# All ten gate pairs of each FFN as seven block products, with some low parts made by an accumulating DMA

## The chip, the core and the metric

The kernel runs on one core of one Trainium2 chip. The metric is device time in microseconds (us) of one launch, median over runs; lower is better.

## The reference, cut to what matters

The program is a trunk of two decoder layers in fp32, on 512 tokens of width 1024. Each layer has four groups of attention heads and then a dense SwiGLU feed-forward network (FFN) of inner width 2816. The change is in the FFN alone:

```python
h = rmsnorm(x, g_pre_ffn[l])
f = jax.nn.silu(jnp.einsum('bsd,df->bsf', h, w_gate[l])) * jnp.einsum('bsd,df->bsf', h, w_up[l])
f = jnp.einsum('bsf,fd->bsd', f, w_down[l])
x = x + rmsnorm(f, g_post_ffn[l])
```

## The kernel before, in words

**Split products.** Every fp32 matrix product is made of three matmuls on operands of type fp32r: each operand is split into a high part (a cast) and a low part (the operand minus its high part), and `mm3` (L195 to L198) adds high by high, high by low and low by high in PSUM. ScalarE (ACT) makes a weight block's high part `whi`, VectorE (DVE) its low part `wlo` (L172 in `weights`, L896 in `split_w`). A raw weight block `wraw` is 256 KB, loaded by a DMA of SyncE's queue (SP); five raw tiles and six `whi` and six `wlo` tiles rotate (WRAW, WSPL).

**The FFN of a layer.** The 2816 inner columns are 22 blocks of 128 (index `j`). Blocks 0 and 1 of gate and up come first, each in two halves of 256 tokens ("the halves"); the last of these four uses a weight tile `w_half` that lies in the tile slot `slotE`. The other 20 blocks are taken in pairs, a gate pair and then an up pair, and then comes the product with `w_down` (`ps_d`).

**A direct pair** is two calls of `block`: 2 x 8 contraction steps x 3 matmuls, 48 matmuls of 512 columns (PSUM tile `ps_g`).

**A pair as seven products** (`two_blocks`): the pair is a 2 x 2 grid of blocks (two halves of the contraction by two weight blocks a11, a12, a21, a22), and seven products p1, p5, p2, p6, p7, p3, p4, in this order, take the place of eight. Each is 4 contraction steps x 3 matmuls of 256 columns, so a pair is 84 (PSUM tile `ps_7`, named `ps` in the profile). Three products take a plain weight block (p1 takes a11, p2 a12, p4 a22); four take a sum s1 to s4, which DVE forms in `combine` (L901). DVE and ACT add the results up (L913, L920, L923). Before the change all ten up pairs of a layer and the five gate pairs with j = 4, 8, 12, 16, 20 go this way; the gate pairs with j = 2, 6, 10, 14, 18 are direct.

**The token side** of products p5, p6, p7 and p4 needs sums T1, T2, T3 and T4 of blocks of h. They are formed once a layer, between the halves and the first pair by seven products, in two rounds c = 0 and c = 1: POOL (GpSimd) adds h's high and low parts back (`back`, L866: b11, b12, b22, b21), DVE forms the differences (L876, L879, L881, L884), and `put` splits them (ACT L871, DVE L872). b11 and b12 have two tiles (NPART), so b12 of round 1 waits until round 0's T3 has been split; T3's tile lies in `slotE` and so waits for the last matmul of the halves.

**What sets the order.** A scheduler that works when the program is built fixes each engine's order; nothing is reordered on the chip. An engine that waits holds up everything behind it in its order.

Of the kernel before, what the change touches and what calls it, by code (L numbers as in the profile page):

```python
# [13 lines left out]
ALU = mybir.AluOpType  # L14
# [62 lines left out]
def f32(ap):  # L77
    return ap.bitcast(F32)
# [3 lines left out]
def decoder(ctx, tc, x, positions, w_in, b_forget, g_mla_q, w_mla_q_up, g_mla_kv, w_mla_kv_up,  # L82
            w_out, g_pre_mix, g_post_mix, w_gate, w_up, w_down, g_pre_ffn, g_post_ffn, consts, out):
    nc = tc.nc
# [5 lines left out]
    ps_mm = ctx.enter_context(tc.tile_pool(name="ps_mm", bufs=3, space=PSUM))  # L90
    ps_s = ctx.enter_context(tc.tile_pool(name="ps_s", bufs=2, space=PSUM))
    ps_t = ctx.enter_context(tc.tile_pool(name="ps_t", bufs=2, space=PSUM))
    ps_o = ctx.enter_context(tc.tile_pool(name="ps_o", bufs=1, space=PSUM))

    def bank(pool, name):
        return pool.tile([P, 512], F32, name=name, tag=pool.name)
# [10 lines left out]
    def H(name):  # L107
        return keep.tile([P, 512], F32, name=name, tag="part", bufs=NPART)
# [46 lines left out]

    chunk_no = [0]
    pool_share = [SHARE_MIX]

    def weights(src, shape, into=None):
        raw = wp.tile([P] + shape, F32, name="wraw", tag="wraw", bufs=WRAW)  # L160
        if into is None:
            hi = wp.tile([P] + shape, F32R, name="whi", tag="whi", bufs=WSPL)
            lo = wp.tile([P] + shape, F32R, name="wlo", tag="wlo", bufs=WSPL)
        else:
            hi, lo = into
        nc.sync.dma_start(raw, src)
        nc.scalar.copy(hi, raw)  # L167
        chunk_no[0] += 1
        if pool_share[0] and chunk_no[0] % pool_share[0] == 0:
            nc.gpsimd.tensor_tensor(lo, raw, f32(hi), op=ALU.subtract)  # L170
        else:
            nc.vector.tensor_tensor(lo, raw, f32(hi), op=ALU.subtract)  # L172
        return hi, lo
# [21 lines left out]
    def mm3(ps, a_hi, a_lo, b_hi, b_lo, start, stop):  # L195
        nc.tensor.matmul(ps, a_hi, b_hi, start=start, stop=False)  # L196
        nc.tensor.matmul(ps, a_hi, b_lo, start=False, stop=False)  # L197
        last_mm[0] = nc.tensor.matmul(ps, a_lo, b_hi, start=False, stop=stop)  # L198
# [620 lines left out]
    def ffn(l, xt, h, turns, f_slots, ahead, after):  # L819
# [5 lines left out]
        def w_of(src, j, into=(None, None)):  # L825
            cs = slice(j * P, (j + 1) * P)
            return [weights(src[l, 4 * i * P:4 * (i + 1) * P, cs].rearrange("(k p) c -> p k c", p=P), [4, P], into=into[i])
                    for i in range(2)]

        def block(ps, w, hs):  # L830
            for k in range(KD):
                hi, lo = w[k // 4]
                mm3(ps[:, hs], hi[:, k % 4, :], lo[:, k % 4, :], h[0][k // 4][:, k % 4, hs], h[1][k // 4][:, k % 4, hs],
                    k == 0, k == KD - 1)
# [52 lines left out]
        def raw_of(src, j, i):  # L887
            raw = wp.tile([P, 4, P], F32, name="wraw", tag="wraw", bufs=WRAW)
            nc.sync.dma_start(raw, src[l, 4 * i * P:4 * (i + 1) * P, j * P:(j + 1) * P].rearrange("(k p) c -> p k c", p=P))
            return raw  # L890

        def split_w(raw):
            hi = wp.tile([P, 4, P], F32R, name="whi", tag="whi", bufs=WSPL)
            lo = wp.tile([P, 4, P], F32R, name="wlo", tag="wlo", bufs=WSPL)
            nc.scalar.copy(hi, raw)  # L895
            nc.vector.tensor_tensor(lo, raw, f32(hi), op=ALU.subtract)  # L896
            return hi, lo

        def combine(a, b, op):
            s = T(F32, "wsum").rearrange("p (k c) -> p k c", c=P)  # L900
            nc.vector.tensor_tensor(s, a, b, op=op)  # L901
            return s

        def product(pool, w, n):
            ps = bank(pool, "ps_7")[:, 0:256]
            for k in range(4):
                mm3(ps, w[0][:, k, :], w[1][:, k, :], ops[n][0][k], ops[n][1][k], k == 0, k == 3)
            return ps

        def two_blocks(src, j, d1, d2):  # L910

            def add(to, a, b):
                nc.vector.tensor_tensor(to, a, b, op=ALU.add)  # L913

            c11, c12, c21, c22 = [d[:, s] for d in (d1, d2) for s in half]
            a11 = raw_of(src, j, 0)
            a21, a22 = raw_of(src, j + 1, 0), raw_of(src, j + 1, 1)
            a12 = raw_of(src, j, 1)
            p1 = product(ps_mm, split_w(a11), "11")
            nc.scalar.copy(c12, p1)  # L920
            s1 = combine(a21, a22, ALU.add)
            p5 = product(ps_s, split_w(s1), "T1")
            nc.scalar.copy(c22, p5)  # L923
            p2 = product(ps_o, split_w(a12), "21")
            add(c11, p2, c12)
            s2 = combine(s1, a11, ALU.subtract)
            p6 = product(ps_mm, split_w(s2), "T2")
            add(c12, p6, c12)
            s3 = combine(a11, a21, ALU.subtract)
            p7 = product(ps_t, split_w(s3), "T3")  # L930
            add(c21, p7, c12)
            s4 = combine(a12, s2, ALU.subtract)
            add(c12, c12, c22)
            add(c22, c22, c21)
            p3 = product(ps_s, split_w(s4), "22")
            add(c12, p3, c12)
            p4 = product(ps_t, split_w(a22), "T4")
            add(c21, p4, c21)

        for j in range(KF):  # L940
            if j < 2:
                (pg, _), (pu, _) = halves[2 * j:2 * j + 2]
            elif j - j % 2 in (4, 8, 12, 16, 20):
                if j % 2 == 0:
                    two_blocks(w_gate, j, fq[j], fq[j + 1])
                pg = fq[j]
            else:
                wg, pg = w_of(w_gate, j), bank(ps_mm, "ps_g")
                block(pg, wg, slice(0, 512))
            f = fq[j]  # L950
            nc.scalar.activation(f, pg, AF.Silu)
            if j < 2:
                nc.vector.tensor_tensor(f, f, pu, op=ALU.mult)
            elif j % 2 == 1:
                u = H("u1"), H("u2")
                two_blocks(w_up, j - 1, *u)
                for i in range(2):
                    f = fq[j - 1 + i]
                    nc.vector.tensor_tensor(f, f, u[i], op=ALU.mult)
# [56 lines left out]
    for c in range(2):  # L1016
        pg = bank(ps_s, "gain")
# [21 lines left out]
    for l in range(depth):  # L1039
# [9 lines left out]
        def after(t, turn):  # L1049
# [7 lines left out]
            if l + 1 < depth:  # L1057
# [9 lines left out]
                nxt_turns[t] = turn_next  # L1067

        ffn(l, xt, h, turns, set_a, ahead, after)
        if nxt:  # L1070
            h = nxt[1]
# [22 lines left out]
```

## Time and profile before

| | us |
|---|---|
| median of 3 runs (1240.09 to 1242.71) | 1241.17 |
| the profiled execution, its own time | 1241.33 |
| its span, first to last instruction | 1239.5 |

The profile's page gives the busy time of each engine over that span. PE is TensorE's matmuls, PEld its weight loads, DVE is VectorE, ACT ScalarE, POOL GpSimd, SP SyncE. A matmul's shown duration overlaps the next one's, so the pitch of matmuls is read from their starts.

### The profile page before, as it was taken

What the parts mean: (1) busy time and instruction counts of PE and PEld (TensorE: products, weight loads), DVE (VectorE), ACT (ScalarE), POOL (GpSimd) and SP (SyncE); (2) the same over time, 40 slices, a digit from 0 to 9 for tenths busy, and PEclk for the clock granted to TensorE, in tenths of its full rate; (3) what the DMA queues carried; (4) which work ended last, traced back from release to release, by engine and by line L of the source; (5) the groups of instructions that cost most, each with busy time, mean ns of one, the idle gap of its engine ahead of it and who ended that gap; (6) DMA issues with size and microseconds to landing.
All of it is one profiled execution on the core that took longest, in us unless ns stands there. A gap on an engine that the chain in (4) does not pass through costs nothing.

```text
span 1239.5 us, 20756 instructions
## 1 busy us (share of the span) xinstructions
PE 1211.5 (98%) x7372; PEld 1069.6 (86%) x7372; DVE 890.6 (72%) x1802; ACT 666.9 (54%) x1453; POOL 245.0 (20%) x337
## 2 busy tenths in 40 slices
PE   8999999989999999999999999999899999999997
PEld 7878877779999999888798888778799999998886
DVE  6877877778987888533667678766788987893334
ACT  6676766754554445332547677666454444453232
POOL 3343444343000000000242434333420000000001
PEclk9999999999999999999999999999999999999999
DMA  7221242521433333533622123233224333343331
GB/s 233 76 61 43 70 117 71 162 68 35 135 96 103 111 103 94 152 95 102 186 84 52 43 69 98 73 116 106 69 69 129 111 94 103 104 117 113 102 91 71
DMA packets 158060, 121.68 MB, mean 98 GB/s; under 512 B 9090, under 2 KB 133122, under 8 KB 157956
## 3 DMA queue, kind: packets, MB, share of 16 engines
q1 hardware_dynamic: 151908, 111.55, 30.9%
q10 hardware_dynamic: 6048, 8.80, 2.7%
q8 instruction: 58, 0.95, 0.3%
q14 instruction: 46, 0.38, 0.1%
HBM read 111.93 MB, written 4.19 MB: 94 GB/s over the span
## 4 chain that ended last, share of the span: by engine, by line
PE 83%; DVE 6%; ACT 4%; issue 2%; DMA 2%; POOL 2%; ACTq 0%; DVEq 0%; POOLq 0%
PE ps L197 8%; PE ps L196 8%; PE ps L198 8%; PE ps_d L197 6%; PE ps_d L198 6%; PE ps_d L196 6%; PE ps_g L197 4%; PE ps_g L196 4%; PE ps_g L198 3%; PE ps_qk L196 3%; PE ps_s L462 3%; PE ps_qk L197 3%; PE ps_qk L198 3%; PE pT L486 2%; PE ps_o L494 1%
## 5 line engine op out<-in xcount | busy, mean ns | idle before, releaser
L172 DVE TENSOR_TENSOR wlo<-wraw,whi 128x512 fp32r<-128x512 f32 x206 | 156.2, 767 | 133.2 <-ACT whi L167 130.7
L167 ACT CAST whi<-wraw 128x512 fp32r<-128x512 f32 (+1 forms) x224 | 135.7, 620 | 170.7 <-PE ps_d L198 117.9
L895 ACT CAST whi<-wsum 128x512 fp32r<-128x512 f32 x120 | 74.3, 620 | 133.4 <-DVE wsum L901 46.5
L197 PE MATMUL ps<-sum,whi 128*128 128x256 f32 x480 | 135.8, 283 | 0.0
L196 PE MATMUL ps<-sum,whi 128*128 128x256 f32 x480 | 135.5, 282 | 0.0
L198 PE MATMUL ps<-sum,wlo 128*128 128x256 f32 x480 | 135.3, 282 | 0.0
L196 PE MATMUL ps_d<-whi,fh 128*128 128x512 f32 x288 | 112.2, 390 | 0.0
L197 PE MATMUL ps_d<-wlo,fh 128*128 128x512 f32 x288 | 112.1, 389 | 0.0
L198 PE MATMUL ps_d<-whi,fl 128*128 128x512 f32 x288 | 112.0, 389 | 0.0
L198 PE MATMUL ps<-h,wlo 128*128 128x256 f32 x360 | 101.9, 283 | 0.0
L197 PE MATMUL ps<-h,whi 128*128 128x256 f32 x360 | 101.9, 283 | 0.0
L196 PE MATMUL ps<-h,whi 128*128 128x256 f32 x360 | 101.8, 283 | 0.0
L477 POOL TENSOR_SCALAR pr<-pr,den 128x128 f32<-128x128 f32 (+3 forms) x128 | 75.7, 608 | 115.1 <-DVE den L474 85.2
L198 PEld LDWEIGHTS ps<-sum,wlo 128*128 128x128 f32 x480 | 91.9, 192 | 0.0
L196 PEld LDWEIGHTS ps<-sum,whi 128*128 128x128 f32 x480 | 91.8, 191 | 0.0
L197 PEld LDWEIGHTS ps<-sum,whi 128*128 128x128 f32 x480 | 91.8, 191 | 0.0
L896 DVE TENSOR_TENSOR wlo<-wsum,whi 128x512 fp32r<-128x512 f32 x120 | 80.9, 683 | 9.5 <-ACT whi L895 8.4
L197 PE MATMUL ps_g<-h,whi 128*128 128x512 f32 (+1 forms) x224 | 81.3, 363 | 5.8 <-DVE h L225 5.8
L196 PE MATMUL ps_g<-h,whi 128*128 128x512 f32 (+1 forms) x224 | 81.1, 363 | 0.9 <-ACT h L225 0.8
L198 PE MATMUL ps_g<-h,wlo 128*128 128x512 f32 (+1 forms) x224 | 80.6, 360 | 0.0
L895 ACT CAST whi<-wraw 128x512 fp32r<-128x512 f32 x90 | 55.8, 620 | 42.6 <-PE ps L197 27.5
L196 PE MATMUL ps_qk<-h,whi 128*128 128x512 f32 x192 | 76.5, 398 | 0.0
(330 smaller groups left out, 3437.8 us busy)
## 6 DMA issues: line engine op xcount, KB each, us to landing
wraw<-in_w_gate_dram SPq DMA_DIRECT2D x88, 256.0 KB, 3.5
wraw<-in_w_up_dram SPq DMA_DIRECT2D x88, 256.0 KB, 3.1
wraw<-in_w_down_dram SPq DMA_DIRECT2D x88, 256.0 KB, 2.9
wraw<-in_w_in_dram SPq DMA_DIRECT2D x72, 256.0 KB, 3.1
wraw<-in_w_out_dram SPq DMA_DIRECT2D x32, 256.0 KB, 2.8
xt<-in_x_dram SPq DMA_DIRECT2D x16, 256.0 KB, 3.7
rope_b<-rope_a ACTq DMA_DIRECT2D x64, 64.0 KB, 2.0
wraw<-in_w_in_dram SPq DMA_DIRECT2D x16, 178.0 KB, 2.9
```

The lines of the kernel that those rows point to most:

```text
L167: nc.scalar.copy(hi, raw)
L172: nc.vector.tensor_tensor(lo, raw, f32(hi), op=ALU.subtract)
L196: nc.tensor.matmul(ps, a_hi, b_hi, start=start, stop=False)
L197: nc.tensor.matmul(ps, a_hi, b_lo, start=False, stop=False)
L198: last_mm[0] = nc.tensor.matmul(ps, a_lo, b_hi, start=False, stop=stop)
L462: nc.tensor.matmul(ps[:, 0:w], a[:, qt * P:(qt + 1) * P], b[:, 0:w], start=i == 0, stop=i == n - 1)
L477: nc.gpsimd.tensor_scalar(p, p, den[:, t - qa:t - qa + 1], 1.0, op0=ALU.mult, op1=ALU.mult)
L486: nc.tensor.transpose(pt[:, i * P:(i + 1) * P], pr[:, offs[qt] + kt * P:offs[qt] + (kt + 1) * P], ident)
L494: nc.tensor.matmul(o, v, mh, start=kt == 0, stop=False)
L895: nc.scalar.copy(hi, raw)
L896: nc.vector.tensor_tensor(lo, raw, f32(hi), op=ALU.subtract)
```

## The change

The five direct gate pairs of each layer become pairs by seven products too, the first of them (j = 2) right behind the halves. And the low part of a plain block in `split_w` is no longer DVE's subtraction: ACT writes the negated high part (raw times -1, rounded to fp32r on writing) into `wlo`, and a DMA issued by POOL adds the raw block onto it.

```diff
+    def low_by_dma(lo, raw):
+        nc.scalar.mul(lo, raw, -1.0)
+        nc.gpsimd.dma_start(lo, raw, accum_op=ALU.add)
...
-        def split_w(raw):
+        def split_w(raw, plain=False):
...
             nc.scalar.copy(hi, raw)
-            nc.vector.tensor_tensor(lo, raw, f32(hi), op=ALU.subtract)
+            if plain:
+                low_by_dma(lo, raw)
+            else:
+                nc.vector.tensor_tensor(lo, raw, f32(hi), op=ALU.subtract)
             return hi, lo
...
-            p1 = product(ps_mm, split_w(a11), "11")
+            p1 = product(ps_mm, split_w(a11, True), "11")
...
-            p2 = product(ps_o, split_w(a12), "21")
+            p2 = product(ps_o, split_w(a12, True), "21")
...
-            p4 = product(ps_t, split_w(a22), "T4")
+            p4 = product(ps_t, split_w(a22, True), "T4")
...
-            elif j - j % 2 in (4, 8, 12, 16, 20):
+            else:
                 if j % 2 == 0:
                     two_blocks(w_gate, j, fq[j], fq[j + 1])
                 pg = fq[j]
-            else:
-                wg, pg = w_of(w_gate, j), bank(ps_mm, "ps_g")
-                block(pg, wg, slice(0, 512))
```

The lines of the changed kernel stand four further down from `low_by_dma` on, so L871, L895, L866 are L875, L899, L870 there.

Where instructions move. First ACT, in layer 0 right behind the halves; sum1 to sum4 are the tiles of T1, T2, T3, T4, `whi` cast from `wsum` is a sum's high part, `whi` from `wraw` a plain block's. Before:

```order
L871 CAST sum3_3519<-b12_3528 128x512
L871 CAST sum1_3518<-t1_3551 128x512
L895 CAST whi_3678<-wsum_3676 128x512
L895 CAST whi_3696<-wraw_3656 128x512
L871 CAST sum3_3519<-b12_3549 128x512
L871 CAST sum2_3520<-b11_3547 128x512
L951 ACTIVATE f_3243<-ps_g_3584 128x512
L871 CAST sum4_3523<-b21_3563 128x512
```

and now:

```order
L875 CAST sum3_3519<-b12_3528 128x512
L927 COPY f_3243<-ps_7_3585 128x256
L875 CAST sum1_3518<-t1_3551 128x512
L899 CAST whi_3601<-wsum_3599 128x512
L899 CAST whi_3619<-wraw_3578 128x512
L875 CAST sum3_3519<-b12_3549 128x512
L875 CAST sum2_3520<-b11_3547 128x512
L875 CAST sum4_3523<-b21_3563 128x512
L160 ACTIVATE wlo_3620<-wraw_3578 128x512
L899 CAST whi_3640<-wsum_3638 128x512
L930 COPY f_3243<-ps_7_3605 128x256
L899 CAST whi_3660<-wsum_3658 128x512
```

The eviction of p1 (L927), the cast of a12 (wraw_3578) and, behind round 1's T casts, the negation of a12 (L160) now stand among the T casts; before, the silu of a direct block stood there.

POOL in the same place, before:

```order
L866 TENSOR_TENSOR b21_3542<-h_2924,h_2926 128x512
L866 TENSOR_TENSOR b11_3547<-h_2923,h_2925 128x512
L866 TENSOR_TENSOR b12_3549<-h_2923,h_2925 128x512
L866 TENSOR_TENSOR b22_3555<-h_2924,h_2926 128x512
L866 TENSOR_TENSOR b21_3563<-h_2924,h_2926 128x512
```

and now:

```order
L870 TENSOR_TENSOR b21_3542<-h_2924,h_2926 128x512
L161 DMA wlo_3581<-wraw_3572 128x512
L870 TENSOR_TENSOR b11_3547<-h_2923,h_2925 128x512
L870 TENSOR_TENSOR b12_3549<-h_2923,h_2925 128x512
L870 TENSOR_TENSOR b22_3555<-h_2924,h_2926 128x512
L870 TENSOR_TENSOR b21_3563<-h_2924,h_2926 128x512
L161 DMA wlo_3620<-wraw_3578 128x512
L161 DMA wlo_3701<-wraw_3576 128x512
```

The accumulating DMA of a11 stands between the two rounds of additions, that of a12 behind the second.

PE right behind p1 of that first pair, now (ps_7_3605 is p5, ps_7_3624 p2, ps_7_3644 p6, ps_7_3664 p7); where nothing but matmuls of the direct pair stood before:

```order
L200 MATMUL ps_7_3605<-sum1_3518,whi_3601 128x256 [waits Activation_49]
L201 MATMUL ps_7_3605<-sum1_3518,whi_3601 128x256 [waits DVE_49]
L200 MATMUL ps_7_3624<-h_2924,whi_3619 128x256 [waits DVE_49,Activation_49]
L201 MATMUL ps_7_3624<-h_2926,whi_3619 128x256
L202 MATMUL ps_7_3605<-sum1_3518,wlo_3602 128x256 [waits DVE_49]
```

and nine matmuls of p5 further on:

```order
L200 MATMUL ps_7_3644<-sum2_3520,whi_3640 128x256 [waits Activation_49]
L201 MATMUL ps_7_3644<-sum2_3521,whi_3640 128x256
L200 MATMUL ps_7_3664<-sum3_3519,whi_3660 128x256 [waits Activation_49]
L202 MATMUL ps_7_3624<-h_2924,wlo_3620 128x256 [waits DMASW1_49]
L200 MATMUL ps_7_3624<-h_2924,whi_3619 128x256
```

PE's third matmul of p5 waits for DVE's low part of s1, and the third of p2 for the accumulating DMA (semaphore DMASW).

## Rows read from the trace of the kernel before

**Rows 1.** The page's parts 1, 2 and 4: engines, granted clock, chain by engine.
```profile
PE 1211.5 (98%) x7372; PEld 1069.6 (86%) x7372; DVE 890.6 (72%) x1802; ACT 666.9 (54%) x1453; POOL 245.0 (20%) x337
...
PEclk9999999999999999999999999999999999999999
...
PE 83%; DVE 6%; ACT 4%; issue 2%; DMA 2%; POOL 2%; ACTq 0%; DVEq 0%; POOLq 0%
```

**Rows 2.** Windows, the stretch of three pairs by seven products, one direct pair before and after.
```profile
348.80:379.00 30.20, 30.20 (x254) 30.20 (x253) 26.64 (x52) 16.12 (x30) 0.00 (x0) 1.00 0.37 107
```

**Rows 3.** Timeline, PE: first matmul of a direct pair, of the sevens, and again.
```profile
296.73 0.40 PE L196 MATMUL ps_g<-h,whi 128*128 128x512 f32 x1
...
307.63 0.28 PE L196 MATMUL ps<-h,whi 128*128 128x256 f32 x1
...
337.79 0.39 PE L196 MATMUL ps_g<-h,whi 128*128 128x512 f32 x1
...
378.85 0.39 PE L196 MATMUL ps_g<-h,whi 128*128 128x512 f32 x1
```

**Rows 4.** Timeline, POOL, layer 0: start us, us, engine, line, operation, [idle before].
```profile
293.51 1.69 POOL L866 TENSOR_TENSOR b<-h 128x512 f32<-128x512 f32 x1 [3.64 <-DVE sum L872]
298.83 4.24 POOL L866 TENSOR_TENSOR b<-h 128x512 f32<-128x512 f32 x3 [3.63 <-DVE sum L872]
```

**Rows 5.** Timeline, DVE, the same stretch.
```profile
297.48 0.67 DVE L953 TENSOR_TENSOR f<-f,ps_u 128x512 f32<-128x512 f32 x1
298.08 0.68 DVE L872 TENSOR_TENSOR sum<-b,sum 128x512 fp32r<-128x512 f32 x1
300.15 1.76 DVE L876 TENSOR_TENSOR t<-b,b 128x512 f32<-128x512 f32 x1 [1.40 <-POOL b L866]
301.84 1.78 DVE L901 TENSOR_TENSOR wsum<-wraw 128x512 f32<-128x512 f32 x1
303.54 0.68 DVE L879 TENSOR_TENSOR b<-b,b 128x512 f32<-128x512 f32 x1
...
305.96 0.69 DVE L884 TENSOR_TENSOR b<-b,b 128x512 f32<-128x512 f32 x1
...
307.16 0.69 DVE L896 TENSOR_TENSOR wlo<-wsum,whi 128x512 fp32r<-128x512 f32 x1
```

**Rows 6.** Timeline, ACT, the same stretch.
```profile
296.98 0.62 ACT L871 CAST sum<-b 128x512 fp32r<-128x512 f32 x1 [0.23 <-PE ps_u L198]
301.95 0.62 ACT L871 CAST sum<-t 128x512 fp32r<-128x512 f32 x1 [4.34 <-DVE t L876]
303.65 0.62 ACT L895 CAST whi<-wsum 128x512 fp32r<-128x512 f32 x1 [1.08 <-DVE wsum L901]
...
304.70 1.38 ACT L871 CAST sum<-b 128x512 fp32r<-128x512 f32 x2
...
306.68 0.62 ACT L871 CAST sum<-b 128x512 fp32r<-128x512 f32 x1
```

**Rows 7.** Timeline, layer 1: POOL, then DVE.
```profile
909.93 4.24 POOL L866 TENSOR_TENSOR b<-h 128x512 f32<-128x512 f32 x3 [3.63 <-DVE sum L872]
...
911.25 1.77 DVE L876 TENSOR_TENSOR t<-b,b 128x512 f32<-128x512 f32 x1 [1.40 <-POOL b L866]
```

**Rows 8.** DMA view from 300 to 500 us, then the page's part 6.
```profile
q1 hardware_dynamic: 38356, 20.20, 35.1%
...
wraw<-in_w_up_dram SPq DMA_DIRECT2D x36, 256.0 KB, 3.0
wraw<-in_w_gate_dram SPq DMA_DIRECT2D x35, 256.0 KB, 3.4
...
rope_b<-rope_a ACTq DMA_DIRECT2D x64, 64.0 KB, 2.0
```

**Rows 9.** Groups by line and shape, ACT.
```profile
L895 ACT CAST whi<-wraw 128x512 fp32r<-128x512 f32 x90 | 55.8, 620 | 42.6 <-PE ps L197 27.5 <-ACT u L920 4.4 <-ACT f L951 4.0
...
L230 ACT ACTIVATE hn<-xt 128x512 f32<-128x512 f32 x32 | 20.2, 631 | 23.9 <-DVE xt L767 14.2 <-DVE xt L998 8.6 <-DMA xt<-in_x_dram 0.9
```

## The prediction

> **What bounds the kernel now.** I first read the page's busy shares, clock and chain: PE is busy 98% of the span at full granted clock and the chain that ends last is 83% PE [rows 1], so time is saved by taking PE work away and lost wherever PE is made to wait. I then went to the stage that changes. A window over three pairs by seven products, 30.20 us long, shows PE busy throughout, DVE 26.64, ACT 16.12 and POOL 0 [rows 2]: PE sets the pace and DVE is near it. The PE timeline gives the prices [rows 3]. A direct pair starts at 296.73 and the first pair by seven products at 307.63, so a direct pair costs 10.9 us; 48 matmuls at a pitch of 0.227 are 10.88. From 307.63 to 337.79 lie three pairs by seven products, so one costs 10.05 us: 84 matmuls at 0.12. The next period, 337.79 to 378.85, is 41.06 = 10.88 + 3 x 10.06.
>
> Last I read what happens between the end of the halves (296.7) and the first pair by seven products (307.6), on POOL, DVE and ACT [rows 4 to 6]. There the T sums are made, and the direct pair is PE's only work meanwhile. The reader is to see how late that chain ends.
>
> **The sum, part by part.**
>
> *PE's work.* Ten direct pairs (five a layer) go, ten by seven products come: 10 x (10.88 - 10.06) = 8.2 us saved, all on the path.
>
> *The head of each layer's pairs.* The first pair by seven products now starts at 296.7 and not at 307.6. p1 needs h and a11 alone, and a11's negation and DMA stand ahead of the wait for the halves' end. p5 then needs T1 and s1. I follow the chain from the rows.
> - ACT casts T3 of round 0 from 296.98, released by the last matmul of the halves [rows 6]; DVE makes its low part from 298.08, behind the product with `ps_u` at 297.48 [rows 5]; POOL's b12, b22, b21 of round 1 run from 298.83 to 303.07 [rows 4]; DVE's T1 difference from 300.15 takes 1.76 beside POOL, s1's sum to 303.6 as much again [rows 5].
> - In the change DVE has no low parts of the direct pair ahead of these, so T3's low part can start at 297.63, when its cast ends: all that follows is 0.45 us earlier.
> - DVE's order keeps s1's low part behind five T steps: 307.16 before [rows 5], now 306.7 to 307.3. PE stands at p5's third matmul until then.
> - ACT negates a12 only behind T4's cast of round 1. That cast waits for DVE's difference at 305.96 [rows 5] and ran at 306.68 [rows 6]; now 306.2 to 306.8, the negation to 307.4. A cast takes 0.62 and an ACTIVATE from SBUF 0.63 [rows 9]. Then POOL's DMA, of length L from issue to landing; p2's third matmul waits for it.
>
> *L is not in the trace.* The nearest rows are plain loads: 64 KB from SBUF to SBUF 2.0 us, 256 KB from HBM 3.0 to 3.4 [rows 8]. Lower end 2.0. Upper end two 256 KB loads one behind the other, 6.8. The DMA reads 256 KB twice, source and destination, so it should be longer than one load: 77 loads (20.2 MB) took 35.1% of 200 us of the engines [rows 8], 0.91 us each; one load plus one such share is 3.4 + 0.9 = 4.3. I take **L = 4.3 us**, an estimate, nearer the single load because both streams are local. The Trainium skill, "DMA: Bandwidth & Descriptors", section "Anatomy of one DMA — SWDGE (gpsimd) path", fits a DMA from the POOL queue as 2.0 us plus bytes at 436 GB/s, an estimate of 2.6 us here and a time of 1253; the loads in the rows are longer than that, and no run here shows one from POOL.
>
> So p2 goes on at 307.4 + 4.3 = 311.7. By then PE has done 29 matmuls of the pair (p1, p5, two each of p2 and p6, one of p7), which end at 296.7 + 29 x 0.12 = 300.2 if nothing waits. **Stall 11.5 us in layer 0.** In layer 1 the same rows stand 611.1 us later (909.93 for 298.83, 911.25 for 300.15) with the same durations and waits [rows 4, 5, 7], and the order of instructions is the same: 2 x 11.5 = 23.0 us lost. With L = 2.0 the low part of a12 is no longer last: two more DVE steps of 0.6 behind 307.3 and ACT's casts of s2 and s3 with an eviction between hold p7 until about 310.1, a stall of 10.0. With 6.8 it is 14.0. The term runs from 20 to 28 us.
>
> *DVE.* 130 low parts go (90 of plain blocks in existing pairs, 40 of direct pairs); ten pairs bring 4 low parts, 4 sums and 7 additions each, 150 instructions. Per pair by seven products, DVE has 26.64 / 3 = 8.9 us now [rows 2] and loses three low parts, some 1.8 at their spacing of 0.6: 7.1 of 10.06. No cost; PE covers it.
>
> *ACT.* 16.12 / 3 = 5.4 us a pair [rows 2], plus three negations at 0.63: 7.3 of 10.06. Covered by PE, unless a negation stands behind a wait as in the head.
>
> *The rotation, pair after pair.* A `whi` tile comes free when its product ends and is needed again five products later, 5 x 1.44 = 7.2 us; cast, negation and L = 4.3 fit (5.6). The tighter loop is a12's raw tile: cast 0.62, negation 0.63, L, then the next pair's a12 is loaded into the same tile, 3.4, with some 0.3 between steps: 4.95 + L against 10.06. It holds up to **L = 5.1**. Loads on SP stand in one queue behind it. So 4.3 leaves 0.8 us, and this step costs nothing.
>
> *POOL.* 120 DMA issues on an engine that is empty here [rows 2]; in the head they stand behind additions that are not late for them.
>
> Sum: 1241.3 (the profiled execution's own time, 0.2 above the median of the runs) - 8.2 + 23.0 = **1256 us**. A stall of 4.1 us a layer would cancel the saving; the chain above, without any DMA, already gives 10.
>
> **Rivals.**
>
> *The accumulating DMA is longer than the rotation allows.* If L passes 5.1, each pair takes 4.95 + L. At L = 6.1 that is 1.0 us on each of the 36 pairs behind the heads, 36, and the heads grow by 2 x 1.8: 1256 + 36 + 4 = 1296. For it: DMA engines now have seven transfers a pair, three of them with two reads, and 35.1% busy becomes some 80 to 90%. Against it: the single loads stand at 3.0 to 3.4 at that share [rows 8]. 22%.
>
> *POOL and DVE hold each other up.* Beside POOL's additions DVE's T1 difference took 1.76 us instead of 0.68 [rows 5]. If an issue waits out one such DVE step, L grows to 6.1 and the time is again 1296; if it only finds DVE's next gap (0.7), L is 5.0 and the time 1257. The Trainium skill, "SBUF — State Buffer", section "SBUF: two separate sides", says that a DMA from the POOL queue has its descriptors written by GpSimd's cores and starves while DVE holds the shared port, 620 ns becoming 3100. By its extra 2.5 us L would be an estimated 6.8 and the time about 1322, but no row here shows a DMA issued by POOL; the page ties the lock to DVE operations in a two-port mode, or with two SBUF inputs against a GpSimd operation that reads SBUF, and the rows show the second kind alone. 8%.
>
> *The head is hidden: faster.* If round 1's T sums were ready before p5, PE would not stop, and the saving stands alone: 1241.3 - 8.2 = 1233. It decides at a stall below 4.1 us a layer, that is p5 and p2 both fed by 304.3 at the latest. For it: the direct pair's work leaves DVE and ACT, and the sums might be made sooner. Against it: the chain hangs on the halves' last matmul through T3's tile, on POOL's 4.24 us behind it and on an order that is fixed [rows 4 to 6]. 6%; a further 3% for a stall between, within 0.2% of no change.
>
> **How the numbers follow.** My forecast, 1256, has 61%; its own range, for L from 2.0 to 5.1, is 1253 to 1258. The long DMA and the port hold 30%, mostly from 1258 to 1305. Faster has 6%, no change 3%. The range 1248 to 1305 leaves out the faster cases and the longest DMAs. 0.2% (2.5 us) is about what a measurement of this kernel can tell from no change: faster 0.06, same 0.03, slower 0.91.
>
> **What would show it.** In the changed profile: a PE gap of some 8 to 9 us in each layer behind p1, released by DVE's `wlo` of s1, and a second of 3 to 4 us released by the DMA; between 320 and 500 us pairs at a pitch of 10.06 with PE busy throughout; landings of 4 to 5 us for `wlo`; POOL's additions of round 1 still from 298.4. It is wrong if PE shows no gap behind the halves (the head was hidden), or if gaps recur in every pair in front of p1, p2 or p4 (the DMA or the port binds).

## The result and the profile after

| | before | after |
|---|---|---|
| median of 4 runs (range), us | 1241.42 (1240.09 to 1242.71) | 1302.35 (1300.05 to 1302.89) |
| the profiled execution, its span | 1239.5 | 1298.0 |

The ratio after to before is 1.0489, 95% interval [1.0476, 1.0502]: 61 us slower, where 15 had been forecast. 1302 lies inside the range, next to its upper end; the forecast's own case (1253 to 1258) did not come about. The upper part of the range stood there for rivals whose mechanisms were not seen either, as shown below, so that the time falls into it is luck.

The page of the changed kernel, parts 1 to 6 in part, against [rows 1]:

```profile
PE 1223.1 (94%) x7732; PEld 1092.7 (84%) x7732; DVE 885.7 (68%) x1822; ACT 746.8 (58%) x1623; POOL 345.6 (27%) x457
...
PE   8999999987998989999999999999789898989997
...
PEclk9999999997999999999999999999979999989999
...
q0 software_dynamic: 17280, 31.46, 15.2%
...
PE 69%; issue 9%; DMA 8%; DVE 7%; ACT 4%; POOL 2%; ACTq 0%; POOLq 0%; DVEq 0%; SPq 0%
...
L908 DVE TENSOR_TENSOR wsum<-wraw 128x512 f32<-128x512 f32 x80 | 57.1, 714 | 72.0 <-DMA wraw<-in_w_gate_dram 36.8
...
wlo<-wraw POOLq DMA_DIRECT2D x120, 256.0 KB, 4.2
```

PE is 94% busy where it was 98%, the granted clock dips three times (behind the halves of each layer and once late in layer 1), and the chain that ended last is 69% PE where it was 83%: DMAs hold 8% of it (the accumulating ones 5%), DVE 7%, and "issue", time in which an engine waited for nothing that the profile shows, 9%. The queue of the accumulating DMAs (q0) moved 31.46 MB in 120 transfers and took 15.2% of the 16 engines' span, 1.64 us of the engines each.

**Behind the halves.** PE's timeline in layer 0, where the direct pair stood before [rows 3]; the first columns are start and duration in us, the brackets tell how long PE waited and for what:

```profile
303.74 0.58 PE L200 MATMUL ps<-sum,whi 128*128 128x256 f32 x1 [5.48 <-ACT whi L899]
...
304.64 0.41 PE L201 MATMUL ps<-h,whi 128*128 128x256 f32 x1
307.32 0.58 PE L202 MATMUL ps<-sum,wlo 128*128 128x256 f32 x1 [2.26 <-DVE wlo L903]
...
310.80 0.58 PE L200 MATMUL ps<-sum,whi 128*128 128x256 f32 x1 [0.55 <-ACT whi L899]
311.19 0.58 PE L202 MATMUL ps<-h,wlo 128*128 128x256 f32 x1
```

p1's last matmul started at 297.98. PE then waited 5.5 us for the high part of s1, 2.3 for its low part, 0.55 for another cast; p2's third matmul came at 311.19. The windows of the same stretch (length, busy time and count for PE, PEld, DVE, ACT, POOL, then granted clock, DMA share, GB/s):

```profile
284.00:296.00 12.00, 11.86 (x97) 11.44 (x96) 8.44 (x10) 6.31 (x10) 7.00 (x5) 1.00 0.13 23
...
302.00:303.00 1.00, 0.00 (x0) 0.00 (x0) 1.00 (x2) 0.02 (x1) 0.49 (x1) 0.88 0.00 0
303.00:304.00 1.00, 0.26 (x1) 0.26 (x2) 1.00 (x3) 0.93 (x2) 0.00 (x0) 0.50 0.00 0
304.00:308.00 4.00, 1.74 (x7) 1.42 (x8) 4.00 (x8) 2.50 (x5) 0.45 (x1) 0.50 0.00 0
308.00:312.00 4.00, 3.45 (x15) 3.05 (x15) 3.49 (x6) 2.76 (x6) 0.43 (x1) 0.50 0.76 159
312.00:316.00 4.00, 4.00 (x20) 4.00 (x20) 1.23 (x4) 2.28 (x5) 1.72 (x2) 0.50 0.87 191
316.00:320.00 4.00, 4.00 (x34) 4.00 (x33) 3.40 (x8) 1.47 (x3) 0.86 (x1) 0.95 0.52 114
320.00:340.00 20.00, 20.00 (x169) 20.00 (x168) 16.34 (x33) 14.30 (x27) 5.16 (x6) 1.00 0.91 190
```

PE stood still from 298.3, and in this halt, between 302 and 303, the granted clock fell to half, 1.2 GHz. It came back only around 316.4. Until then matmuls of 256 columns started every 0.21 us and not every 0.12 (20 rows from 312 to 316): what PE did from 303.7 to 316.4 it did at half speed.

**Then once in most gate and up periods.** The pairs do not run at a pitch of 10.06 as in [rows 2, 3]. In layer 0 PE waits for an accumulating DMA in front of p4 of eight of the ten up pairs, 0.6 to 2.8 us each time. One such place, PE and then ACT, DVE and POOL before it:

```profile
352.04 0.39 PE L202 MATMUL ps<-sum,wlo 128*128 128x256 f32 x1 [2.75 <-DMA wlo<-wraw]
```

```profile
344.56 0.63 ACT L955 ACTIVATE f<-f 128x512 f32<-128x512 f32 x1 [2.36 <-DVE f L920]
345.10 0.35 ACT L927 COPY u<-ps 128x256 f32<-128x256 f32 x1
345.35 0.62 ACT L899 CAST whi<-wraw 128x512 fp32r<-128x512 f32 x1
345.87 0.63 ACT L160 ACTIVATE wlo<-wraw 128x512 fp32r<-128x512 f32 x1
```

```profile
343.50 0.69 DVE L908 TENSOR_TENSOR wsum<-wraw 128x512 f32<-128x512 f32 x1 [1.88 <-DMA wraw<-in_w_gate_dram]
344.11 0.42 DVE L920 TENSOR_TENSOR f<-ps,f 128x256 f32<-128x256 f32 x1
```

```profile
346.80 0.86 POOL L161 DMA_DIRECT2D wlo<-wraw  x1 [7.60 <-ACT wlo L160]
```

```profile
341.90 4.88 issue
346.80 5.20 DMA wlo<-wraw
352.04 0.39 PE ps L202
```

Read backwards: PE waits 2.75 us until 352.04 for a22's low part. The DMA was issued at 346.80 and landed 5.2 us later, counted from the start of its issue, behind a negation that began at 345.87 (L160). The chain view names only "issue" before the DMA; POOL's row names the negation. In ACT's order that negation stands behind the silu of the gate pair (L955). The silu waited 2.36 us until 344.56 for DVE's last addition (L920 at 344.11). DVE in turn stood at a sum of the *next* pair (L908) whose raw block landed only at 343.50. And this is what the loads stand behind, SP's queue (waits from 330 to 500 us: total, times, longest):

```profile
SPq L893 <- DMA wlo<-wraw: 93.7, 44, 5.3
SPq L893 <- DVE wsum L908: 41.7, 14, 3.7
```

SP waited 94 us in 170 for accumulating DMAs to have read a raw tile, before it could issue the next load into that tile. The longest of these waits, 5.3 us, is for the very DMA followed here: SP's next load went out at 352.0, when that DMA had landed. The total alone proves little, since an SP that waits costs nothing as long as the loads land in time: in raw_spare below, 33 us faster, SP waits 103 us for such DMAs. The sign of late loads is DVE's wait for them. Over the run DVE's sums waited 72 us (the row of L908 above), nearly all for loads; from 330 to 500 us it was 36 us, and 3.6 in dve_lows, which has no accumulating DMA.

That DMA was a long one. At the seven other such places of layer 0 it landed 3.7 to 3.8 us after its issue began, less than the 4.3 of the forecast, and PE waited all the same, because it was issued late. The next place, POOL and then PE:

```profile
369.13 0.86 POOL L161 DMA_DIRECT2D wlo<-wraw  x1 [7.62 <-ACT wlo L160]
```

```profile
372.95 0.39 PE L202 MATMUL ps<-sum,wlo 128*128 128x256 f32 x1 [0.55 <-DMA wlo<-wraw]
```

### The profile page after: what moved, and what is told of

It is laid out like the page before. It is cut to its first block, busy times and chain, and to the rows that moved or that the text cites. A ratio compares the mean times of both kernels' runs of the same rounds, so it can differ in the third digit from the quotient of the medians.

```text
span 1298.0 us, 22186 instructions
## 1 busy us (share of the span) xinstructions
PE 1223.1 (94%) x7732; PEld 1092.7 (84%) x7732; DVE 885.7 (68%) x1822; ACT 746.8 (58%) x1623; POOL 345.6 (27%) x457
## 3 DMA queue, kind: packets, MB, share of 16 engines
q0 software_dynamic: 17280, 31.46, 15.2%
## 4 chain that ended last, share of the span: by engine, by line
PE 69%; issue 9%; DMA 8%; DVE 7%; ACT 4%; POOL 2%; ACTq 0%; POOLq 0%; DVEq 0%; SPq 0%
PE ps L202 8%; PE ps L200 7%; PE ps L201 7%; PE ps_d L201 6%; PE ps_d L202 6%; PE ps_d L200 6%; DMA wlo<-wraw 5%; PE ps_s L466 3%; PE ps_qk L200 2%; PE ps_qk L201 2%; PE ps_qk L202 2%; PE pT L490 2%; PE ps_out L202 1%; PE ps_v L201 1%; POOL pr L481 1%
## 5 line engine op out<-in xcount | busy, mean ns | idle before, releaser
L176 DVE TENSOR_TENSOR wlo<-wraw,whi 128x512 fp32r<-128x512 f32 (+1 forms) x166 | 128.7, 785 | 130.9 <-ACT whi L171 130.5
L202 PE MATMUL ps<-sum,wlo 128*128 128x256 f32 x640 | 185.8, 290 | 31.9 <-DMA wlo<-wraw 27.3
L171 ACT CAST whi<-wraw 128x512 fp32r<-128x512 f32 x184 | 111.7, 620 | 154.7 <-PE ps_d L202 119.1
L200 PE MATMUL ps<-sum,whi 128*128 128x256 f32 x640 | 184.6, 288 | 12.1 <-ACT whi L899 12.1
L161 POOL DMA_DIRECT2D wlo<-wraw x120 | 103.6, 870 | 346.4 <-ACT wlo L160 179.1
L201 PE MATMUL ps<-sum,whi 128*128 128x256 f32 x640 | 183.8, 287 | 0.0
L899 ACT CAST whi<-wsum 128x512 fp32r<-128x512 f32 x160 | 96.4, 616 | 71.4 <-issue 28.3
L200 PE MATMUL ps<-h,whi 128*128 128x256 f32 x480 | 137.4, 286 | 0.0
L201 PE MATMUL ps<-h,whi 128*128 128x256 f32 x480 | 137.2, 286 | 0.0
L200 PEld LDWEIGHTS ps<-sum,whi 128*128 128x128 f32 x640 | 125.6, 196 | 13.1 <-ACT whi L899 13.1
L201 PEld LDWEIGHTS ps<-sum,whi 128*128 128x128 f32 x640 | 125.6, 196 | 0.0
L908 DVE TENSOR_TENSOR wsum<-wraw 128x512 f32<-128x512 f32 x80 | 57.1, 714 | 72.0 <-DMA wraw<-in_w_gate_dram 36.8
L202 PEld LDWEIGHTS ps<-h,wlo 128*128 128x128 f32 x480 | 93.4, 195 | 4.3 <-DMA wlo<-wraw 3.9
L201 PEld LDWEIGHTS ps<-h,whi 128*128 128x128 f32 x480 | 93.5, 195 | 0.0
L200 PEld LDWEIGHTS ps<-h,whi 128*128 128x128 f32 x480 | 93.3, 194 | 0.0
```

The source lines that it names most:

```text
L161: nc.gpsimd.dma_start(lo, raw, accum_op=ALU.add)
```

## The experiments

The times fall into three parts: PE's work, the stall behind the halves ("the head"), and what comes back in each period. In the names of the kernels "spare" stands for two raw tiles more, "behind" for a forced place of the silu; both are shown below. In the table "gate pairs" counts those by seven products a layer, and "rest" is what is left over PE's work, 1241.4 less 0.82 for each such pair beyond five a layer [rows 3]. Each ratio is against the kernel before measured beside that kernel (medians of 1240.3 to 1241.9), so "rest" is good to about 1 us.

| kernel | gate pairs | low parts of a11, a12, a22 | median us | ratio to before, 95% interval | rest |
|---|---|---|---|---|---|
| the change | 10 | DMA | 1302.4 | 1.0489 [1.0476, 1.0502] | 69 |
| dve_lows | 10 | DVE | 1258.3 | 1.0134 [1.0115, 1.0154] | 25 |
| first_direct_dma | 9 | DMA | 1279.2 | 1.0307 [1.0287, 1.0328] | 44 |
| five_direct_dma | 5 | DMA | 1247.5 | 1.0049 [1.0034, 1.0064] | 6 |
| first_direct_dve | 9 | DVE | 1267.7 | 1.0205 [1.0190, 1.0221] | 33 |
| raw_spare | 10 | DMA | 1269.7 | 1.0233 [1.0215, 1.0251] | 36 |
| silu_behind | 10 | DMA | 1272.4 | 1.0249 [1.0229, 1.0269] | 39 |
| raw_spare_behind | 10 | DMA | 1263.5 | 1.0186 [1.0171, 1.0201] | 30 |
| pool_lows | 10 | POOL | 1345.9 | 1.0847 [1.0829, 1.0866] | 113 |
| first_direct_dma_spare | 9 | DMA | 1250.7 | 1.0085 [1.0070, 1.0100] | 16 |
| first_direct_dve_spare | 9 | DVE | 1253.8 | 1.0108 [1.0088, 1.0128] | 19 |
| a22_dma_spare | 9 | a22 DMA | 1245.2 | 1.0039 [1.0027, 1.0051] | 10 |
| a22_dma_spare_behind | 9 | a22 DMA | 1239.2 | 0.9986 [0.9977, 0.9995] | 4 |
| first_direct_dve_spare_behind | 9 | DVE | 1255.3 | 1.0099 [1.0083, 1.0114] | 20 |
| two_direct_dve_spare | 8 | DVE | 1237.0 | 0.9967 [0.9956, 0.9978] | 0.5 |

### Which half of the change costs what

```diff
- split_w(a11, True), split_w(a12, True), split_w(a22, True)
+ split_w(a11), split_w(a12), split_w(a22)            (dve_lows, first_direct_dve)
...
-            else:
+            elif j - j % 2 not in (2,):        (first_direct_*; five_direct_dma: 2, 6, 10, 14, 18)
...
+            else:
+                wg, pg = w_of(w_gate, j), bank(ps_mm, "ps_g")
+                block(pg, wg, slice(0, 512))
```

dve_lows. 

> All twenty pairs a layer by seven products as in the change, but every low part is DVE's subtraction again: no negation, no accumulating DMA. Loop theory (the changed kernel's time is three terms: -8.2 us of PE work, 13.2 us of stall behind the halves in each layer, and about 43 us of stalls that come back once in each gate and up period because a low part by negation and DMA takes 5.5 us in place of 0.6): only the first two are left, 1241.4 - 8.2 + 26.4 = 1260, and PE pairs stand at a pitch of 10.06 without gaps behind the first pair. Full-DVE theory (what comes back is a want of DVE time that the direct pairs used to give, 8.9 to 9.2 of 10.06 us busy): the gaps stay, now released by DVE, and the time is 1280 or more.

first_direct_dma. 

> The change with one difference: the first gate pair of each layer (j = 2) stays direct. Head theory: PE goes on behind the halves, its granted clock stays up, and both layers' 13.2 us of stall go, while two pairs cost 0.82 more each: 1302.4 - 26.4 + 1.6 = 1278. The stalls that come once a period stay (eight gate pairs a layer still stand before up pairs). If the head is really paid elsewhere (the same wait one pair later), the time stays above 1290.

dve_lows gave 1258.3. Taking the accumulating DMA out of the changed kernel brings back 1302.4 - 1258.3 = **44 us**, and what is left over PE's work is 25 us. first_direct_dma gave 1279.2, so one direct pair ahead in each layer takes away 23 us and 1.6 of saved work, **12.4 a layer for the head** ((23.1 + 1.6) / 2). The two runs agree on the split to a few us. By the rows of layer 0 the second pair starts 13.4 us late in the changed kernel (at 320.15, where 296.66 + 10.06 = 306.7 was due) and 11.4 us late in dve_lows; in layer 1 it is 13.8 and 11.5. So about 4 of the 44 us lie in the two heads, and some 40 in the pairs behind them. The clock in the head, windows of first_direct_dma, then of dve_lows:

```profile
296.00:304.00 8.00, 8.00 (x47) 7.08 (x47) 6.16 (x8) 3.98 (x9) 5.60 (x5) 1.00 0.58 148
```

```profile
304.00:312.00 8.00, 5.46 (x23) 5.15 (x24) 6.82 (x12) 4.11 (x9) 0.00 (x0) 0.50 0.04 12
```

With a direct pair for PE to do meanwhile, the clock stays at full; without that pair it is at half, also in the kernel without any accumulating DMA.

five_direct_dma. 

> The five direct gate pairs of each layer stay direct, as in the kernel before; only the low parts of a11, a12 and a22 in the 30 pairs by seven products go to the negation and the accumulating DMA. Head theory: behind the halves PE has no gap and keeps its clock. Loop theory: the stall comes back only where a gate pair by seven products stands before an up pair (4 or 5 of 10 periods a layer), about half of 43 us: 1241.4 + 20 = 1261. If the length of the DMA alone were the cause, each of the 30 pairs would lose about 1 us wherever it stands: 1271, with gaps behind direct pairs too. If the direct pairs' longer PE time and fewer transfers give the loop its slack back: 1241 to 1245.

It gave 1247.5, near the lowest of the three cases written: the same DMA on 30 pairs (15 a layer) costs only 6 us as long as every second gate pair is direct. It takes no fixed amount per pair, and the loss belongs to the two halves of the change together.

first_direct_dve. 

> The first gate pair of each layer direct, the other nineteen pairs by seven products, every low part DVE's subtraction. Loop and head theory together: neither stall is left and PE does eight pairs at 0.82 us less, 1241.4 - 6.6 = 1234.8, faster than both kernels. Full-DVE theory: a pair asks about 9 us of DVE in a row of 10.06 us pairs with no direct pair between, waits for DVE come up in each period, and the time is 1241 or more.

It gave 1267.7, 33 us over PE's work: a miss. Even without the DMA nineteen pairs in a row lose time here, and the DMA version with the same pairs (first_direct_dma, 1279.2) is only 11.5 us slower. So the 44 us hold for the changed kernel and are not the price of the DMA in every order. Waits of DVE and of PE in this kernel, 330 to 500 us:

```profile
DVE wsum L908 <- DMA wraw<-in_w_up_dram: 12.8, 8, 2.5
DVE wsum L908 <- DMA wraw<-in_w_gate_dram: 4.6, 7, 1.5
```

```profile
PE ps L202 <- DVE wlo L903: 8.6, 6, 2.0
```

DVE, 90% busy there (152.6 of 170 us), waits for raw blocks and PE waits for DVE. Why dve_lows, with the same work in the pairs, has next to no such waits (PE waited 0.8 us in the same stretch, with DVE 96% busy, 162.6 of 170 us) was not settled; a full DVE alone does not explain it. Its order on DVE differs, and the head holds PE up by some 11.5 us in each layer, which may give the loads a lead; the two were not told apart.

### The raw tiles

In raw_spare a22 is loaded into one of two free tiles of `fq` (22 of 24 are used), so that five rotating tiles serve three blocks a pair.

```diff
-        def raw_of(src, j, i):
-            raw = wp.tile([P, 4, P], F32, name="wraw", tag="wraw", bufs=WRAW)
+        def raw_of(src, j, i, spare=False):
+            if spare:
+                raw = fq[KF + pair_no[0] % 2].rearrange("p (k c) -> p k c", c=P)
+            else:
+                raw = wp.tile([P, 4, P], F32, name="wraw", tag="wraw", bufs=WRAW)
...
-            a21, a22 = raw_of(src, j + 1, 0), raw_of(src, j + 1, 1)
+            a21, a22 = raw_of(src, j + 1, 0), raw_of(src, j + 1, 1, pair_no[0] >= 1)
+            pair_no[0] += 1
```

> The changed kernel with two raw tiles more: a22 of each pair by seven products (the first pair of a layer apart) is loaded into one of two tiles that nobody else uses, in turn, and so a11, a21 and a12 have the five rotating tiles for themselves. Raw-tile theory (a raw tile is held until the accumulating DMA has read it, so SP issues the next loads late, DVE waits for them, and a22's negation comes late): the stalls that come back in each period go, the head's 26 us stay: 1302.4 - 43 = 1260, up to 1270 if some stay. Silu theory (a22's cast and negation stand behind the gate pair's silu in ACT's order and wait for the gate pair's last addition, whenever the load is there): the stalls stay, 1290 to 1305. Bandwidth theory (DMA engines 80 to 90% busy make every transfer late): no gain either, 1295 to 1305, with landings above 4 us.

It gave 1269.7, 32.7 us less, with the DMA, its length and its share of the engines about unchanged. DMA view of raw_spare, 330 to 500 us, then of the changed kernel:

```profile
q0 software_dynamic: 7033, 12.80, 47.4%
...
wlo<-wraw POOLq DMA_DIRECT2D x32, 256.0 KB, 4.6
...
wlo<-f POOLq DMA_DIRECT2D x17, 256.0 KB, 3.8
```

```profile
q0 software_dynamic: 6550, 11.91, 44.3%
...
wlo<-wraw POOLq DMA_DIRECT2D x45, 256.0 KB, 4.4
```

The engines are as full (47.4% for the accumulating DMAs in place of 44.3%) and a landing takes 4.6 us for blocks in rotating tiles and 3.8 for a22 (`wlo<-f`), in place of 4.4, and still the time falls: a full set of DMA engines is not what binds. Held raw tiles are one link of what does; a22 was given the two tiles, and tiles for other blocks were not tried. The build changed the order on ACT and DVE in places too, but at the places looked at the silu still stands in front of a22's cast and negation; it waits 17.3 us for DVE's additions from 330 to 500 us, where it waited 29.2.

first_direct_dma_spare. 

> The change with the first gate pair of a layer direct (1279.2 with five raw tiles) and the two raw tiles more for a22: no stall behind the halves, and DVE relieved by the accumulating DMA. Raw-tile theory: 1241.4 - 6.6 = 1235, at most 1245. Silu theory and bandwidth theory: the stalls of each period stay, 1270 to 1280.

first_direct_dve_spare. 

> The first gate pair of a layer direct, nineteen pairs by seven products, low parts by DVE (1267.7 with five raw tiles, where DVE waited 17 us in 170 for loads and PE then for DVE), with the two raw tiles more for a22. Raw-tile theory: loads come early, DVE's 9 us in 10.06 suffice: 1241.4 - 6.6 = 1235. Full-DVE theory (DVE has too little room without direct pairs between, loads early or not): 1255 to 1268.

They gave 1250.7 and 1253.8: 29 and 14 us less than with five raw tiles, but 16 and 19 us over PE's work and so short of what was written. The tiles are most of the loss with the DMA (29 of 44 us) and less than half of it without (14 of 33).

### The silu's place

silu_late. 

> The changed kernel with the silu of a gate pair put behind the up pair's products, so that in ACT's order no wait for the gate pair's last addition stands before the casts and negations of the up pair. Silu theory: the stall before p4 of each up pair goes, 1302.4 - 43 = 1260. Raw-tile theory: SP still waits for the accumulating DMAs to free raw tiles and DVE for the loads, the stall moves to another place or stays, 1285 to 1305. Bandwidth theory: 1295 to 1305.

It gave 1299.7. The build's scheduler had put the silu back: on all five engines the order of that kernel is the changed kernel's, row for row. The run tested nothing but repetition (0.2% from 1302.4). silu_behind forces the order instead:

```diff
+            last_act[0] = nc.scalar.copy(hi, raw)     (and the negation in low_by_dma)
...
+                    with tc.issue_after(last_act[0].ins):
+                        nc.scalar.activation(f, f, AF.Silu)
                     nc.vector.tensor_tensor(f, f, u[i], op=ALU.mult)
```

silu_behind. 

> The changed kernel with the silu of a gate pair forced behind the up pair's a22 negation in ACT's order (in the earlier run with the silu written later, the build had put it back in its old place, and that kernel's order was the changed kernel's own). Silu theory: the stall in front of the up pairs' p4 goes, 1302.4 - 43 = 1260. Raw-tile theory: the loads still wait for the accumulating DMAs; the silu is a link of the chain but not the one that binds, 1285 to 1300. Both: the chain needs late loads and the silu, either cure gives most of it, 1265 to 1275.

raw_spare_behind. 

> The changed kernel with the two extra raw tiles for a22 (1269.7) and the silu forced behind a22's negation. What is left there above head and PE work alone (1241.4 - 8.2 + 26.4 = 1259.6) is 10 us of waits for a22's DMA in front of p4 of up pairs. Silu theory for that rest: 1258 to 1262. If the rest is the DMA's own length or loads that are still late: 1266 to 1272.

They gave 1272.4, as written for two links together, and 1263.5, between the two cases. Against the changed kernel that is -30.0 for the order alone, -32.7 for the tiles alone, -38.9 for both, of 44. ACT's waits for the gate pair's addition in the changed kernel and in silu_behind (where L966 is the silu), and PE's waits, all from 330 to 500 us:

```profile
ACT f L955 <- DVE f L920: 29.2, 15, 3.4
```
```profile
ACT f L966 <- DVE f L922: 4.2, 6, 1.2
```

```profile
PE ps L202 <- DMA wlo<-wraw: 11.6, 9, 2.7
```
```profile
PE ps L204 <- DMA wlo<-wraw: 3.8, 5, 1.7
```

The chain read above has two links, the late load and the silu in front of the negation, and needs both: take either away and most of it goes. In silu_behind the loads are still late (DVE waits 32 us for them, in place of 36), and PE hardly stops. With both gone 5 us stay over dve_lows. Some 4 of them are the longer heads (the second pair of layer 0 starts 13.6 us late, in dve_lows 11.4), and PE's waits for landings behind the heads come to 1.6 us.

pool_lows. 

> The changed kernel, but POOL makes the low parts of a11, a12 and a22 by one subtraction (1.45 us for such a block in the kernel before) where negation, issue and DMA took 5.5. DVE is as relieved as in the change, ACT has no negation, and a raw tile is free 4 us earlier. Raw-tile theory: the stalls of each period go, the head stays: 1302.4 - 43 = 1260. If POOL and DVE hold each other up (DVE's difference took 1.76 in place of 0.68 beside POOL's additions), 4.4 us of POOL a pair cost DVE some 2 to 4 us and it is over 9 of 10.06 busy: 1265 to 1300, with DVE's two-input operations above 0.9 us on the mean.

```diff
-        nc.scalar.mul(lo, raw, -1.0)
-        nc.gpsimd.dma_start(lo, raw, accum_op=ALU.add)
+        nc.gpsimd.tensor_tensor(lo, raw, f32(hi), op=ALU.subtract)
```

It gave 1345.9, outside everything written. Whether a raw tile came free sooner at all is not shown. Groups by line on DVE, and POOL's and ACT's waits from 330 to 500 us:

```profile
L902 DVE TENSOR_TENSOR wlo<-wsum,whi 128x512 fp32r<-128x512 f32 x160 | 124.9, 785 | 9.8 <-ACT whi L898 9.7
L907 DVE TENSOR_TENSOR wsum<-wraw 128x512 f32<-128x512 f32 x80 | 66.5, 831 | 98.1 <-DMA wraw<-in_w_up_dram 64.9 <-DMA wraw<-in_w_gate_dram 33.3
```
```profile
POOL wlo L160 <- ACT whi L898: 106.4, 21, 12.2
```
```profile
ACT f L954 <- DVE f L919: 37.2, 13, 6.0
```

DVE's subtraction takes 785 ns and its sum 831, where the changed kernel has 683 and 714: POOL and DVE do slow each other, though less than feared. Larger is that ACT's casts stand behind the silu (waits up to 6.0 us) and POOL behind those casts (up to 12.2 us). PE, for its part, waited 52.0 us over the run for DVE's low parts of sums and 4.0 us for POOL's low parts. It may be the same link by another road, but that was not shown: how much of the 1346 is each was not tried apart.

### Is there a version that gains

```diff
-            p1 = product(ps_mm, split_w(a11, True), "11")
+            p1 = product(ps_mm, split_w(a11), "11")          (a22_dma_spare; a12 alike, a22 stays)
...
-            elif j - j % 2 not in (2,):
+            elif j - j % 2 not in (2, 12):                   (two_direct_*)
```

a22_dma_spare. 

> First gate pair of a layer direct; a22 in the two extra raw tiles, and its low part alone by negation and accumulating DMA, those of a11 and a12 by DVE. The DMA then holds no tile of the rotation, and DVE has one low part a pair less (8.3 in place of 8.9 of 10.06). Raw-tile theory: the least stall of all versions with nineteen such pairs, 1235 to 1245. If the length of the accumulating DMA itself is the cost (p4 waits for it): PE gaps in front of p4 as before, 1250 or more.

a22_dma_spare_behind. 

> First gate pair of a layer direct, a22 in the extra tiles with its low part alone by DMA (1245.2, where PE still waited for that DMA in front of p4 of up pairs), and the silu forced behind a22's negation. Silu theory for the rest: those waits go, 1235 to 1238, faster than before. Otherwise 1243 to 1247.

first_direct_dve_spare_behind. 

> One direct pair a layer, low parts by DVE, extra tiles for a22, silu forced behind a22's cast (1253.8 without that order). If the silu's place was the rest of the loss: 1241.2 - 6.6 = 1235. If DVE, at 8.9 of 10.06, is too full without direct pairs between: 1245 to 1254, and the accumulating DMA's relief (1239.2 with a22 by DMA) is worth the difference.

1245.2, 1239.2 and 1255.3. With the head hidden, the tiles added and the silu moved, one accumulating DMA a pair is worth 14 to 16 us against DVE doing the same low part (by the ratios, and as 1255.3 - 1239.2). DVE's share does not tell the two apart: it is busy 158.3 of 170 us from 330 to 500 without the DMA and 158.0 with it. PE's waits do: over the run 4.4 us for DVE's low parts and 6.9 for its additions in front of `ps_d` without the DMA, 1.5 us for the DMA with it. So the accumulating DMA is no bad trade by itself; it needs its wait covered.

two_direct_dve_spare. 

> Two gate pairs of a layer direct (j = 2 and j = 12), eighteen by seven products, low parts by DVE, a22 in the two extra raw tiles. A direct pair is one in which DVE has little to do: theory of a DVE that runs full and falls behind slowly (what is left in the version with one direct pair, 1253.8): half of its 19 us of stall goes, 1241.4 - 4.9 + 10 = 1246. If the second direct pair lets it recover fully: 1236.5, faster than before.

five_direct_spare. 

> The kernel before (five direct gate pairs a layer, all low parts by DVE) with nothing but the two extra raw tiles for a22. PE had no wait for a low part in its pairs there, so both theories say 1241, within 2 us; were it 1237 or less, the gain of the version with two direct pairs (1237.0) would come from the tiles and not from PE work saved.

two_direct_dve_spare gave **1237.0, ratio 0.9967 [0.9956, 0.9978]: faster than both kernels**. The tiles alone give the kernel before nothing (five_direct_spare: 1242.3, ratio 1.0014 [1.0005, 1.0023]), so the 3.8 us are PE's work: 4.9 were expected for three more gate pairs a layer, and PE waits almost nowhere. Its page and PE's waits from 296 to 520 us:

```profile
span 1236.1 us, 21336 instructions
...
PE 1205.5 (98%) x7588; PEld 1076.1 (87%) x7588; DVE 924.0 (75%) x1886; ACT 679.9 (55%) x1483; POOL 243.7 (20%) x337
```
```profile
PE ps L202 <- DVE wlo L908: 0.3, 1, 0.3
```

Two variants of it did no better.

two_direct_dve_spare_behind. 

> Two direct pairs a layer, low parts by DVE, extra tiles, silu forced behind a22's cast (1237.0 without that order). PE work alone: 1241.2 - 4.9 = 1236.3; nothing was left to cure but 1 us of waits: 1235.5 to 1237.5.

two_direct_a22_dma_spare_behind. 

> The same with the low part of a22 by the accumulating DMA in place of DVE. If the DMA's length is covered: 1236.3, the same as without it; if p4 still waits for it in some pairs, as in the version with one direct pair (1239.2 against 1234.6 of PE work): 1238 to 1241.

They gave 1238.4, ratio 0.9972 [0.9960, 0.9984], and 1241.0, ratio 0.9992 [0.9984, 1.0001]: where DVE keeps up, the DMA gives nothing.

## Why the prediction was right about the sign and wrong about the size

- **PE's work, -8.2: held as far as it was measured.** In two_direct_dve_spare, with three gate pairs more a layer and hardly a wait, 4.9 were due and 3.8 came.
- **The head, 11.5 a layer: the chain held, the clock was missing.** 12.4 by first_direct_dma, 13.4 by the rows of layer 0. The ends of the chain stand where they were put (s1's low part by DVE at 307.32, forecast 307.3; p2's third matmul at 311.19, forecast 311.7, with the 29 matmuls done that were counted: 11.0 us late). But p5's first wait was for ACT's cast of s1. And PE worked at half the clock, which the forecast did not have: PE was not idle while a12's DMA ran, it was still at p5 and p6 (0.55 us of wait there where 3 to 4 had been named). Up to 311.19 a full clock would have gained little, since that DMA, issued at 307.55, landed only 3.6 us later. Behind it, to 316.47, 24 matmuls took 5.3 us where 24 x 0.12 = 2.9: these 2.4 us are the clock's (an estimate from these rows). Without any DMA the prediction's chain gives 10 a layer, 1253; dve_lows measured 1258.3, with 11.4 in layer 0.
- **"So 4.3 leaves 0.8 us, and this step costs nothing": the step that failed.** It stood at nothing and cost some 40 us (the 44 less the 4 in the heads). The length was not the error. It counts from the start of the issue on POOL, and its median is 4.2 to 4.4 us, as forecast; the single values run from 3.3 to 6.0, with 8 of 54 over the step's limit of 5.1 between 320 and 520 us, but of the eight DMAs that PE waited for in front of p4 in layer 0 seven took 3.7 to 3.8. What failed is the path: the step followed a12's tile around one loop and asked only whether that loop closes. The tile that held SP up in the place read above is a22's, whose DMA is the last of its pair and whose landing SP's next load waits for (352.0 above). And the real loop passes through three queues in which nothing overtakes: SP, where each load stands behind the wait of the load before it; DVE, where a sum of the next pair stands ahead of an addition of this one; and ACT, where the silu stands ahead of a22's cast and negation. Taking away the first link (raw_spare) brings back 32.7 us, the last (silu_behind) 30.0, both 38.9. The sentence on ACT said "unless a negation stands behind a wait" and looked for that in the head alone.
- **DVE and ACT, no cost: right about their time, wrong as an argument.** DVE has less to do, as forecast, but it waits for loads; ACT waits for DVE.
- **First rival (a DMA longer than the rotation allows), 1296: nearest.** It named "in front of p1, p2 or p4" as its sign, and p4 it is, in most up pairs. Its mechanism, L at 6.1 and 1 us on each pair, is not what was seen: the median L is 4.2 to 4.4, PE waits 0.6 to 2.8 us once in most periods of layer 0, and the loss is only 6 us in all when direct pairs stand between (five_direct_dma). That its time came close is luck.
- **Second rival (POOL and DVE hold each other up): not seen for the DMA.** All 54 issues between 320 and 520 us took 859 to 862 ns, and DVE's subtraction 683 on the mean. What this rival fears does exist, as pool_lows shows, but for POOL's arithmetic. The issue rows:

```profile
L161 POOL DMA_DIRECT2D wlo<-wraw x54: 859/859/862, 324.4 to 515.2; - x54
...
DMA to landing us min/median/max: 3.3/4.3/6.0
```

The Trainium skill, "SBUF — State Buffer", section "SBUF: two separate sides", lets the descriptors of such a DMA starve while DVE holds the shared port; with an issue time this constant and landings of 3.3 to 6.0 us, this trace shows no sign of it. The estimate of 2.6 us from "DMA: Bandwidth & Descriptors" in the Trainium skill, section "Anatomy of one DMA — SWDGE (gpsimd) path", lies under every landing in these rows.

- **Third rival (a hidden head): no.** The head is exposed in all kernels with the first pair by seven products that were looked at.

## What to carry to other kernels

When an operation becomes longer but leaves a busy engine, do not only ask whether its own loop closes: list for each queue it touches (loads, ACT, DVE) what stands behind each wait, and follow one late transfer through all of them. Its length can be as forecast and the engine behind it still wait, because it was issued late. And an edit in the source that is meant to move an instruction proves nothing until the built order shows that it moved.

## What was not expected of the hardware

- **Half the clock around a short halt.** PE stood still for 5.5 us, and from within this halt until about 316.4 it was granted 0.50, with matmuls every 0.21 us for 0.12. Of layer 0's head of 13.4 us, 2.4 are put down to it above.
- **What an accumulating DMA takes.** A 256 KB transfer added onto SBUF took 1.64 us of the 16 engines (15.2% of 1298 us over 120), a plain load of that size some 0.9 [rows 8]. With seven transfers a pair the engines are 80% busy between 320 and 520 us, and 83% in raw_spare, which is 33 us faster: their share is not what slows the changed kernel.
